# Rotary embedding on one core: two tiles rotated by POOL, eight added by it, five summed by TensorE, and VectorE at full tile width throughout

## The chip, the core and the metric

The kernel runs on one core of a Trainium2 chip. The core has TensorE (PE), VectorE (DVE), ScalarE (ACT), GpSimd (POOL) and SyncE (SP), which run their own instruction streams and wait for one another by semaphores. Data moves between the main memory (HBM), the on-chip memory SBUF and TensorE's accumulators (PSUM); 16 DMA engines carry the HBM traffic. Transfers here are issued from two queues: SP's, shown as q1, and ACT's, shown as q10. The metric is the device time in microseconds of one execution, and the median of several is compared.

## The reference

The input `x` has the shape (8, 8, 1024, 64) in float32, and the tables `cos_cached` and `sin_cached` have the shape (1024, 32). Each row of 64 is rotated as two halves of 32:

```python
x_first, x_second = x[:, :, :, :half], x[:, :, :, half:]
out_first = x_first * cos_cached - x_second * sin_cached
out_second = x_first * sin_cached + x_second * cos_cached
```

An output element is thus a product with the cosine, plus or minus a product of the other half with the sine.

## The kernel before

`x` is cut into 16 tiles, numbered 0 to 15. A tile is 128 partitions by 2048 elements (32 rows of 64), or 1 MB. All tiles have their own place in SBUF (`xt`), and results overwrite them. The loads are issued at once from SP's queue: tiles 0 and 1 alone (L64), then pairs. Before them go the sine table on SP (L57) and the cosine table on ACT (L58). The tables are spread to 128 partitions twice: to PSUM (`snp` by VectorE, `csp` by ScalarE, L72 and L73), where VectorE's products read them, and within SBUF (`sn`, `cs`, by POOL, L76), where POOL's own products read them.

A tile takes one of four ways:

- `on_pool`: POOL does two products (L87, L88) and two half-tile additions (L92, L93), and SP stores.
- `vector_pool`: VectorE does the two products, with the sine product in a `vs` buffer, POOL does the two additions, and SP stores. Tile 12's additions and store are cut in two halves.
- `vector_tensor`: VectorE does the two products; TensorE adds them by multiplying with the identity matrix `plus` and its negative `minus`, into the PSUM tile `acc` (L115, L116), 16 rows at a time; ScalarE copies the sums back to SBUF (L118) and issues the store from ACT's queue.
- `vector_alone`: VectorE does all four operations on half a tile (L132 to L135). Its sine product lies in an `acc` buffer in PSUM, and ACT issues the store.

The order is written out by hand (`manual_schedule`), one call after another; each engine executes its share in that order. `vector_tensor` gets tiles 0, 2, 5, 8 and 11; `on_pool` 1, 6 and 9; `vector_pool` 3, 4, 7, 10 and 12. Tile 13 is split: TensorE sums its first half, and `vector_alone` does its second. Tiles 14 and 15 are `vector_alone`, in halves.

There are six `vs` buffers for the sine products (`tv`), one `gs` buffer for POOL's (`tg`), and two `acc` buffers of 16 rows in PSUM (`pa`). A buffer is written again only when its last readers are done. A store waits for its tile's last writer and, where it uses a semaphore that an earlier transfer had, for that one.

Of the kernel before, what the change touches and what calls it, by code (L numbers as in the profile page):

```python
# [8 lines left out]
@with_exitstack  # L9
def kernel(  # L10
    ctx: ExitStack,
    tc: tile.TileContext,
    x: bass.AP,
    cos_cached: bass.AP,
    sin_cached: bass.AP,
    out: bass.AP,
):
    nc = tc.nc
    fp32 = mybir.dt.float32
    TT = mybir.AluOpType  # L20
    P = nc.NUM_PARTITIONS

    b, h, seq, hd = x.shape
    half = hd // 2
    R = 32
    F = R * hd
    T = R * half
    Q = seq // R
    reps = P // Q
    n_ch = (b * h * seq) // (R * P)  # L30
    G = 512 // half
    assert seq % R == 0 and P % Q == 0 and Q % 32 == 0

    xf = x.rearrange("b h s d -> (b h s d)").rearrange(
        "(c p m) -> c p m", p=P, m=F)
    of = out.rearrange("b h s d -> (b h s d)").rearrange(
        "(c p m) -> c p m", p=P, m=F)

    ctx.enter_context(tc.manual_schedule())
    const = ctx.enter_context(tc.tile_pool(name="const", bufs=1))  # L40
    xp = ctx.enter_context(tc.tile_pool(name="xp", bufs=1))
    tv = ctx.enter_context(tc.tile_pool(name="tv", bufs=6))
    tg = ctx.enter_context(tc.tile_pool(name="tg", bufs=1))
    pt = ctx.enter_context(
        tc.tile_pool(name="pt", bufs=1, space=bass.MemoryType.PSUM))
    pa = ctx.enter_context(
        tc.tile_pool(name="pa", bufs=2, space=bass.MemoryType.PSUM))

    cs = const.tile([P, T], fp32, name="cs")
    sn = const.tile([P, T], fp32, name="sn")  # L50
    plus = const.tile([P, P], fp32, name="plus")
    minus = const.tile([P, P], fp32, name="minus")
    csp = pt.tile([P, T], fp32, name="csp")
    snp = pt.tile([P, T], fp32, name="snp")


    nc.sync.dma_start(out=sn[0:Q], in_=sin_cached.rearrange("(p n) j -> p (n j)", p=Q))  # L57
    nc.scalar.dma_start(out=cs[0:Q], in_=cos_cached.rearrange("(p n) j -> p (n j)", p=Q))  # L58


    xt = []
    for first, n in [(0, 1), (1, 1)] + [(c, 2) for c in range(2, n_ch, 2)]:
        t = xp.tile([P, n, F], fp32, name=f"x{first}")
        nc.sync.dma_start(out=t, in_=xf[first:first + n].rearrange("c p m -> p c m"))  # L64
        xt += [t[:, i] for i in range(n)]

    for t, v in ((plus, 1.0), (minus, -1.0)):
        nc.gpsimd.memset(t, 0.0)
        nc.gpsimd.affine_select(out=t, in_=t, compare_op=TT.not_equal, fill=v,
                                base=0, pattern=[[-1, P]], channel_multiplier=1)  # L70
    for r in range(reps):
        nc.vector.tensor_copy(out=snp[r * Q:(r + 1) * Q], in_=sn[0:Q])  # L72
        nc.scalar.copy(out=csp[r * Q:(r + 1) * Q], in_=cs[0:Q])  # L73
    for t in (sn, cs):
        for r in range(1, reps):
            nc.gpsimd.tensor_copy(out=t[r * Q:(r + 1) * Q], in_=t[0:Q])  # L76

    def rows(t, n0=0, n1=R):
        return t[:, n0 * hd:n1 * hd].rearrange("p (n k j) -> p n k j", k=2, j=half)

    def tab(t, n0=0, n1=R):
        v = t[:, n0 * half:n1 * half].rearrange("p (n o j) -> p n o j", o=1, j=half)
        return v.to_broadcast([P, n1 - n0, 2, half])

    def products(eng, c, s, ctab, stab):
        xr = rows(xt[c])
        eng.tensor_tensor(out=rows(s), in0=xr, in1=tab(stab), op=TT.mult)  # L87
        eng.tensor_tensor(out=xr, in0=xr, in1=tab(ctab), op=TT.mult)  # L88

    def sums(eng, c, s, n0, n1):  # L90
        xr, sr = rows(xt[c], n0, n1), rows(s, n0, n1)
        eng.tensor_tensor(out=xr[:, :, 0], in0=xr[:, :, 0], in1=sr[:, :, 1], op=TT.subtract)  # L92
        eng.tensor_tensor(out=xr[:, :, 1], in0=xr[:, :, 1], in1=sr[:, :, 0], op=TT.add)  # L93

    def store(q, c, n0=0, n1=R):
        q.dma_start(out=of[c][:, n0 * hd:n1 * hd], in_=xt[c][:, n0 * hd:n1 * hd])

    def on_pool(c):
        s = tg.tile([P, F], fp32, name="gs")
        products(nc.gpsimd, c, s, cs, sn)  # L100
        sums(nc.gpsimd, c, s, 0, R)
        store(nc.sync, c)

    def vector_pool(c, cuts=(0, R)):
        s = tv.tile([P, F], fp32, name="vs")
        products(nc.vector, c, s, csp, snp)
        for n0, n1 in zip(cuts, cuts[1:]):
            sums(nc.gpsimd, c, s, n0, n1)
            store(nc.sync, c, n0, n1)

    def tensor_sums(c, s, n0):
        xr, sr = rows(xt[c], n0, n0 + G), rows(s, n0, n0 + G)
        acc = pa.tile([P, 2, G, half], fp32, name="acc")
        for k in range(2):
            nc.tensor.matmul(acc[:, k], plus, xr[:, :, k], start=True, stop=False)  # L115
            nc.tensor.matmul(acc[:, k], plus if k else minus, sr[:, :, 1 - k],  # L116
                             start=False, stop=True)
        nc.scalar.copy(out=xr, in_=acc.rearrange("p k n j -> p n k j"))  # L118

    def vector_tensor(c):  # L120
        s = tv.tile([P, F], fp32, name="vs")
        products(nc.vector, c, s, csp, snp)
        for n0 in range(0, R, G):
            tensor_sums(c, s, n0)
        store(nc.scalar, c)

    def vector_alone(c, n0):
        n1 = n0 + G
        xr = rows(xt[c], n0, n1)
        s = pa.tile([P, 2, G, half], fp32, name="acc")  # L130
        sr = s.rearrange("p k n j -> p n k j")
        nc.vector.tensor_tensor(out=sr, in0=xr, in1=tab(snp, n0, n1), op=TT.mult)  # L132
        nc.vector.tensor_tensor(out=xr, in0=xr, in1=tab(csp, n0, n1), op=TT.mult)  # L133
        nc.vector.tensor_tensor(out=xr[:, :, 0], in0=xr[:, :, 0], in1=s[:, 1], op=TT.subtract)  # L134
        nc.vector.tensor_tensor(out=xr[:, :, 1], in0=xr[:, :, 1], in1=s[:, 0], op=TT.add)  # L135

    vector_tensor(0)
    on_pool(1)
    vector_tensor(2)
    vector_pool(3)  # L140
    vector_pool(4)
    on_pool(6)
    vector_tensor(5)
    vector_pool(7)
    vector_tensor(8)
    on_pool(9)
    vector_pool(10)
    vector_tensor(11)
    vector_pool(12, (0, G, R))


    s = tv.tile([P, F], fp32, name="vs")
    xr, sr = rows(xt[13], 0, G), rows(s, 0, G)
    nc.vector.tensor_tensor(out=sr, in0=xr, in1=tab(snp, 0, G), op=TT.mult)
    nc.vector.tensor_tensor(out=xr, in0=xr, in1=tab(csp, 0, G), op=TT.mult)
    tensor_sums(13, s, 0)
    vector_alone(13, G)
    store(nc.scalar, 13)
    for c in (14, 15):
        for n0 in range(0, R, G):  # L160
            vector_alone(c, n0)
            store(nc.scalar, c, n0, n0 + G)

# [1 line left out]
_INS = ['x', 'cos_cached', 'sin_cached']  # L165
# [26 lines left out]
```

## Time and profile before

| What | Value |
|---|---|
| Median of 4 runs | 86.16 us (85.98 to 86.93) |
| Profiled execution | 85.98 us |
| Its span | 84.0 us |
| Bytes moved | 33.82 MB, mean 402 GB/s over the span |
| PE busy | 42.1 us, 50% |
| VectorE busy | 70.7 us, 84% |
| ACT busy | 16.5 us, 20% |
| POOL busy | 71.7 us, 85% |
| DMA share of q1 and q10 | 72.8% and 24.2% |

The busy times are those of the profiled execution, and the shares are of its span. The span runs from the program's first instruction to its last; the execution's time beside it contains what lies around it. A slice of the span is 2.1 us. The DMA share is the mean busy share of the 16 engines.

### The profile page before, as it was taken

To read this page: it belongs to the slowest core of one execution; us is meant where nothing else is said; L and a number is where in the kernel's file an instruction comes from. 1 tells how busy PE (TensorE), PEld (TensorE's weight loads), DVE (VectorE), ACT (ScalarE), POOL (GpSimd) and SP (SyncE) were. 2 spreads that over 40 slices of the span, in tenths; PEclk is the share of its full clock that TensorE was granted. 3 is DMA by queue.
4 is the path that set the end of the run, shared out by engine and by line. 5 is a ranking of instruction groups with operands and counts; after the bars stand their busy time and mean duration, and the time that the engine had idled before them with its cause. 6 is when DMAs were issued, how large, how long until landed. Compare 5 with 4: busy or idle time off the path is not lost.

```text
span 84.0 us, 396 instructions
## 1 busy us (share of the span) xinstructions
PE 42.1 (50%) x88; PEld 17.6 (21%) x88; DVE 70.7 (84%) x46; ACT 16.5 (20%) x16; POOL 71.7 (85%) x38
## 2 busy tenths in 40 slices
PE   0000007999999708995599829999960000000000
PEld 0000004344444104440344214444400000000000
DVE  0399997999999999999999999990599999999400
ACT  4397000013404220044004130040431000000000
POOL 5399999999999999999999999999999999960000
PEclk9999999999999999999999995699998555555555
DMA  1999999999999999999999999999999999999992
GB/s 41 333 437 433 421 402 433 433 433 406 413 433 316 429 429 417 437 437 429 417 421 437 417 437 437 425 421 421 437 413 437 437 425 421 411 435 409 417 423 88
DMA packets 5024, 33.82 MB, mean 402 GB/s; under 512 B 480, under 2 KB 480, under 8 KB 1312
## 3 DMA queue, kind: packets, MB, share of 16 engines
q1 hardware_dynamic: 3536, 25.30, 72.8%
q10 hardware_dynamic: 1488, 8.52, 24.2%
HBM read 17.04 MB, written 16.78 MB: 402 GB/s over the span
## 4 chain that ended last, share of the span: by engine, by line
PE 46%; DVE 32%; issue 6%; ACT 5%; DMA 3%; DVEq 1%
PE acc L115 24%; PE acc L116 22%; DVE x L133 7%; DVE acc L132 7%; DVE snp L72 6%; ACT x L118 5%; DVE x L134 3%; DMA sn<-in_sin_cached_dram 3%; DVE x L135 3%; DVE vs L87 3%; DVE x L88 3%; DVEq L187 1%; DVEq L88 0%
## 5 line engine op out<-in xcount | busy, mean ns | idle before, releaser
L115 PE MATMUL acc<-x,plus 128*128 128x512 f32 x44 | 24.6, 643 | 20.1 <-DVE x L88 13.2
L87 DVE TENSOR_TENSOR vs<-x,snp 128x2048 f32<-128x2048 f32 x10 | 22.8, 2281 | 0.5 <-DMA x<-in_x_dram 0.5
L88 DVE TENSOR_TENSOR x<-x,csp 128x2048 f32<-128x2048 f32 x10 | 22.9, 2287 | 0.4
L118 ACT COPY x<-acc 128x1024 f32<-128x1024 f32 x11 | 11.1, 1013 | 44.2 <-PE acc L116 44.2
L115 PEld LDWEIGHTS acc<-x,plus 128*128 128x128 f32 x44 | 8.7, 205 | 32.1 <-issue 26.6
L88 POOL TENSOR_TENSOR x<-x,cs 128x2048 f32<-128x2048 f32 x3 | 13.6, 4531 | 0.2
L87 POOL TENSOR_TENSOR gs<-x,sn 128x2048 f32<-128x2048 f32 x3 | 13.6, 4545 | 0.1
L116 PE MATMUL acc<-vs,minus 128*128 128x512 f32 x22 | 12.9, 670 | 0.0
L93 POOL TENSOR_TENSOR x<-x,vs 128x1024 f32<-128x1024 f32 (+1 forms) x6 | 12.0, 1996 | 0.0
L92 POOL TENSOR_TENSOR x<-x,vs 128x1024 f32<-128x1024 f32 (+1 forms) x6 | 11.9, 1992 | 0.0
L116 PE MATMUL acc<-vs,plus 128*128 128x512 f32 x22 | 11.2, 592 | 0.0
L132 DVE TENSOR_TENSOR acc<-x,snp 128x1024 f32<-128x1024 f32 x5 | 6.1, 1225 | 3.1 <-ACT x L118 3.1
L72 DVE COPY snp<-sn 32x1024 f32<-32x1024 f32 x4 | 4.9, 1223 | 3.5 <-DMA sn<-in_sin_cached_dram 3.4
L92 POOL TENSOR_TENSOR x<-x,gs 128x1024 f32<-128x1024 f32 x3 | 7.1, 2352 | 0.2
L93 POOL TENSOR_TENSOR x<-x,gs 128x1024 f32<-128x1024 f32 x3 | 7.1, 2353 | 0.0
L133 DVE TENSOR_TENSOR x<-x,csp 128x1024 f32<-128x1024 f32 x5 | 6.1, 1221 | 0.2
L116 PEld LDWEIGHTS acc<-vs,minus 128*128 128x128 f32 x22 | 4.6, 210 | 6.0 <-issue 6.0
L116 PEld LDWEIGHTS acc<-vs,plus 128*128 128x128 f32 x22 | 4.3, 197 | 5.6 <-issue 5.6
L76 POOL COPY sn<-sn 32x1024 f32<-32x1024 f32 x3 | 3.1, 1032 | 1.8 <-DMA sn<-in_sin_cached_dram 1.7
L73 ACT COPY csp<-cs 32x1024 f32<-32x1024 f32 x4 | 4.0, 1008 | 1.4 <-DMA cs<-in_cos_cached_dram 1.3
L134 DVE TENSOR_TENSOR x<-x,acc 128x512 f32<-128x512 f32 x5 | 3.4, 687 | 0.2
L135 DVE TENSOR_TENSOR x<-x,acc 128x512 f32<-128x512 f32 x5 | 3.4, 679 | 0.0
(12 smaller groups left out, 8.2 us busy)
## 6 DMA issues: line engine op xcount, KB each, us to landing
x<-in_x_dram SPq DMA_DIRECT2D x7, 2048.0 KB, 26.5
out_dram<-x SPq DMA_DIRECT2D x7, 1024.0 KB, 16.2
out_dram<-x ACTq DMA_DIRECT2D x6, 1024.0 KB, 9.0
x<-in_x_dram SPq DMA_DIRECT2D x2, 1024.0 KB, 6.0
out_dram<-x ACTq DMA_DIRECT2D x4, 512.0 KB, 7.1
out_dram<-x SPq DMA_DIRECT2D x2, 512.0 KB, 7.1
cs<-in_cos_cached_dram ACTq DMA_DIRECT2D x1, 128.0 KB, 3.0
sn<-in_sin_cached_dram SPq DMA_DIRECT2D x1, 128.0 KB, 2.7
```

Of the source, the lines that this page charges most:

```text
L72: nc.vector.tensor_copy(out=snp[r * Q:(r + 1) * Q], in_=sn[0:Q])
L87: eng.tensor_tensor(out=rows(s), in0=xr, in1=tab(stab), op=TT.mult)
L88: eng.tensor_tensor(out=xr, in0=xr, in1=tab(ctab), op=TT.mult)
L92: eng.tensor_tensor(out=xr[:, :, 0], in0=xr[:, :, 0], in1=sr[:, :, 1], op=TT.subtract)
L93: eng.tensor_tensor(out=xr[:, :, 1], in0=xr[:, :, 1], in1=sr[:, :, 0], op=TT.add)
L115: nc.tensor.matmul(acc[:, k], plus, xr[:, :, k], start=True, stop=False)
L116: nc.tensor.matmul(acc[:, k], plus if k else minus, sr[:, :, 1 - k], start=False, stop=True)
L118: nc.scalar.copy(out=xr, in_=acc.rearrange("p k n j -> p n k j"))
L132: nc.vector.tensor_tensor(out=sr, in0=xr, in1=tab(snp, n0, n1), op=TT.mult)
L133: nc.vector.tensor_tensor(out=xr, in0=xr, in1=tab(csp, n0, n1), op=TT.mult)
L134: nc.vector.tensor_tensor(out=xr[:, :, 0], in0=xr[:, :, 0], in1=s[:, 1], op=TT.subtract)
L135: nc.vector.tensor_tensor(out=xr[:, :, 1], in0=xr[:, :, 1], in1=s[:, 0], op=TT.add)
```

## The change

The split of the tiles is made anew, and no half-width operation of VectorE is left. `on_pool` gets tiles 1 and 6; `vector_pool` gets 2, 3, 5, 8, 10, 12, 13 and 14, of which 14 is added and stored in two halves; `vector_tensor` gets 0, 4, 7, 9 and 11. Tile 15 is the only one of `vector_alone`, which now works on a whole tile and issues one store of 1 MB from ACT's queue. The two `acc` buffers become one tile of 128x2048 in PSUM, of which TensorE uses one half (16 rows) after the other; tile 15's sine product lies in all of it. `minus` is made by ScalarE from `plus` instead of by POOL. The order in which the loads are issued stays, as do the six `vs` buffers.

```diff
-        tc.tile_pool(name="pa", bufs=2, space=bass.MemoryType.PSUM))
+        tc.tile_pool(name="pa", bufs=1, space=bass.MemoryType.PSUM))
...
+    acc = pa.tile([P, F], fp32, name="acc")
...
-    for t, v in ((plus, 1.0), (minus, -1.0)):
-        nc.gpsimd.memset(t, 0.0)
-        nc.gpsimd.affine_select(out=t, in_=t, compare_op=TT.not_equal, fill=v,
-                                base=0, pattern=[[-1, P]], channel_multiplier=1)
+    nc.gpsimd.memset(plus, 0.0)
+    nc.gpsimd.affine_select(out=plus, in_=plus, compare_op=TT.not_equal, fill=1.0,
+                            base=0, pattern=[[-1, P]], channel_multiplier=1)
+    nc.scalar.mul(minus, plus, -1.0)
...
     def vector_tensor(c):
         s = tv.tile([P, F], fp32, name="vs")
         products(nc.vector, c, s, csp, snp)
         for n0 in range(0, R, G):
-            tensor_sums(c, s, n0)
+            xr, sr = rows(xt[c], n0, n0 + G), rows(s, n0, n0 + G)
+            a = acc[:, n0 * hd:(n0 + G) * hd].rearrange("p (k n j) -> p k n j", k=2, j=half)
+            for k in range(2):
+                nc.tensor.matmul(a[:, k], plus, xr[:, :, k], start=True, stop=False)
+                nc.tensor.matmul(a[:, k], plus if k else minus, sr[:, :, 1 - k],
+                                 start=False, stop=True)
+            nc.scalar.copy(out=xr, in_=a.rearrange("p k n j -> p n k j"))
         store(nc.scalar, c)
 
-    def vector_alone(c, n0):
...
+    def vector_alone(c):
+        products(nc.vector, c, acc, csp, snp)
+        sums(nc.vector, c, acc, 0, R)
+        store(nc.scalar, c)
 
     vector_tensor(0)
     on_pool(1)
-    vector_tensor(2)
+    vector_pool(2)
     vector_pool(3)
-    vector_pool(4)
+    vector_tensor(4)
     on_pool(6)
-    vector_tensor(5)
-    vector_pool(7)
-    vector_tensor(8)
-    on_pool(9)
+    vector_pool(5)
+    vector_tensor(7)
+    vector_pool(8)
+    vector_tensor(9)
     vector_pool(10)
     vector_tensor(11)
-    vector_pool(12, (0, G, R))
...
+    vector_pool(12)
+    vector_pool(13)
+    vector_pool(14, (0, G, R))
+    vector_alone(15)
```

More of the change, by code (lines that the diff above doesn't have):

```diff
@@ L109, in vector_pool @@
             store(nc.sync, c, n0, n1)
[L111 to L118, printed above, removed]
     def vector_tensor(c):
@@ L123, in vector_tensor @@
         for n0 in range(0, R, G):
-            tensor_sums(c, s, n0)
-        store(nc.scalar, c)
-    def vector_alone(c, n0):
[L128 to L135, printed above, removed]
+            xr, sr = rows(xt[c], n0, n0 + G), rows(s, n0, n0 + G)
[5 more added lines that the diff above has]
+            nc.scalar.copy(out=xr, in_=a.rearrange("p k n j -> p n k j"))
+        store(nc.scalar, c)
+    def vector_alone(c):
+        products(nc.vector, c, acc, csp, snp)
+        sums(nc.vector, c, acc, 0, R)
+        store(nc.scalar, c)
     vector_tensor(0)
     on_pool(1)
-    vector_tensor(2)
+    vector_pool(2)
     vector_pool(3)
-    vector_pool(4)
+    vector_tensor(4)
     on_pool(6)
-    vector_tensor(5)
-    vector_pool(7)
-    vector_tensor(8)
-    on_pool(9)
+    vector_pool(5)
+    vector_tensor(7)
+    vector_pool(8)
+    vector_tensor(9)
     vector_pool(10)
     vector_tensor(11)
-    vector_pool(12, (0, G, R))
[L152 to L162, printed above, removed]
+    vector_pool(12)
+    vector_pool(13)
+    vector_pool(14, (0, G, R))
+    vector_alone(15)
 _INS = ['x', 'cos_cached', 'sin_cached']
```

## The prediction

> **What bounds the kernel now.** I read the slices first, then the queues, and only then the engines.
>
> ```profile
> DMA  1999999999999999999999999999999999999992
> GB/s 41 333 437 433 421 402 433 433 433 406 413 433 316 429 429 417 437 437 429 417 421 437 417 437 437 425 421 421 437 413 437 437 425 421 411 435 409 417 423 88
> DMA packets 5024, 33.82 MB, mean 402 GB/s; under 512 B 480, under 2 KB 480, under 8 KB 1312
> ```
>
> The 16 DMA engines are full from the second slice to the last but one. No compute engine looks like that over the whole span. The table of windows shows how the end is reached:
>
> ```profile
> core 0: us, PE busy (x) PEld busy (x) DVE busy (x) ACT busy (x) POOL busy (x), PEclk, DMA share, GB/s
> 28.00:64.00 36.00, 27.29 (x58) 11.00 (x57) 32.57 (x19) 8.10 (x8) 35.69 (x13) 0.95 1.01 427
> 72.00:76.00 4.00, 0.00 (x0) 0.00 (x0) 3.93 (x5) 0.00 (x0) 2.82 (x3) 0.50 1.02 425
> 76.00:80.00 4.00, 0.00 (x0) 0.00 (x0) 2.56 (x4) 0.00 (x0) 0.00 (x0) 0.50 1.02 417
> ...
> 81.00:82.00 1.00, 0.00 (x0) 0.00 (x0) 0.00 (x0) 0.00 (x0) 0.00 (x0) 0.50 1.02 418
> 82.00:83.00 1.00, 0.00 (x0) 0.00 (x0) 0.00 (x0) 0.00 (x0) 0.00 (x0) 0.50 0.40 160
> ```
>
> VectorE, the last engine to work, stops at 78.6 us, but the DMA engines stay full until 82.5 us. The last landing is at 83.08 us, and 0.95 us of closing work completes the span of 84.03 us. The steady rate is 427 GB/s, or 0.427 MB per us. The 33.82 MB alone need 79 us of it. The change moves exactly the same bytes. So it can gain next to nothing while the queues stay fed, and it loses where it leaves them empty.
>
> The chain of waits says otherwise, and is the view to distrust here:
>
> ```profile
> PE 46%; DVE 32%; issue 6%; ACT 5%; DMA 3%; DVEq 1%
> ```
>
> It follows compute instructions back from VectorE's last one, and cannot show that their stores waited in a full queue.
>
> **The unit prices.**
>
> ```profile
> L87 DVE TENSOR_TENSOR vs<-x,snp 128x2048 f32<-128x2048 f32 x10 | 22.8, 2281 | 0.5 <-DMA x<-in_x_dram 0.5
> L88 DVE TENSOR_TENSOR x<-x,csp 128x2048 f32<-128x2048 f32 x10 | 22.9, 2287 | 0.4
> L87 POOL TENSOR_TENSOR gs<-x,sn 128x2048 f32<-128x2048 f32 x3 | 13.6, 4545 | 0.1
> L134 DVE TENSOR_TENSOR x<-x,acc 128x512 f32<-128x512 f32 x5 | 3.4, 687 | 0.2
> ```
>
> In the timeline VectorE takes a new tile's products every 4.52 us (two operations that overlap by 0.05). POOL takes a whole tile in 13.8 us (10.03 to 23.84) and the two additions of a tile in 4.6 us (46.95 to 51.55).
>
> **POOL: three whole tiles and five tiles of sums become two and eight.** Removed: one whole tile, 13.8 us. Added: three times 4.6, also 13.8. Before, POOL's tile work ran from 10.03 to 74.81; it still ends at about 74.8. Its order becomes 1, 2, 3, 6, 5, 8, 10, 12, 13, 14: adds end at 51.55 (tile 5), 56.15, 60.75, 65.35, 69.95, and tile 14's halves at 72.4 and 74.8. The unneeded memset and select for `minus` (0.5 us) end before POOL's wait for `sn` at 3.5, so taking them away gives nothing.
>
> **ScalarE: makes `minus` by one 128x128 multiplication.** No such row exists. Between 0 and the 1.01 us of the 128x1024 copy, I take 0.3. It falls between the table load's end at 2.46 and the cosine table's landing at 3.75; if it overran, `csp` at 7.9 would still be 2.9 us ahead of its first use at 10.85. Cost 0.
>
> **TensorE: five and a half tiles of sums become five.** Half a tile goes: four matmuls in two passes each, 8 x 0.43 = 3.4 us in the timeline, and one 1.01 us copy. With it goes VectorE's wait for that copy:
>
> ```profile
> 59.85 1.23 DVE L132 TENSOR_TENSOR acc<-x,snp 128x1024 f32<-128x1024 f32 x1 [3.08 <-ACT x L118]
> ```
>
> From the end of a product to the issue of its ACT store takes 8.2 us (31.79 to 40.07), 10.0 where the clock was halved (49.87 to 59.85). The single `acc` with two halves holds as much PSUM as the two buffers did. Tiles 4, 7 and 9 are ready at 27.25, 36.3 and 45.3, so PE is free before each: no new wait.
>
> **VectorE: 14 full products and one addition.** Gone are five half-width groups of four operations and one half-width pair. Tile 0 runs as before, to 13.14; tile 2 starts at 13.62. Then 2, 3, 4, 5, 7, 8, 9, 10 follow every 4.52 us, and tile 11 would start at 49.78. It does not. There are six `vs` buffers, and in the built program tile 11's first product waits for POOL's last addition of tile 5, whose buffer it takes over. POOL reaches that here:
>
> ```profile
> 46.95 2.34 POOL L92 TENSOR_TENSOR x<-x,vs 128x1024 f32<-128x1024 f32 x1
> 49.24 2.34 POOL L93 TENSOR_TENSOR x<-x,vs 128x1024 f32<-128x1024 f32 x1
> 51.55 4.52 POOL L87 TENSOR_TENSOR gs<-x,sn 128x2048 f32<-128x2048 f32 x1
> ```
>
> So the change adds a wait of 1.8 us. The balance: removed are 5 x 3.75 for the half-width groups, 2.45 for the pair and the wait of 3.08, 24.3 in all; added are four tiles of 4.52, two additions of about 1.2 (below) and 1.8, 22.3 in all. VectorE comes out 2.0 earlier. Behind it stand tiles 11 to 15 on VectorE; PE's sums of 11 and POOL's of 12 to 14 wait for those. Products of 11, 12, 13, 14 and 15 then end at 56.1, 60.6, 65.1, 69.65 and 74.2. POOL wants 12 at 60.75, 13 at 65.35 and 14 at 69.95, so it gets each just in time. Tile 15's two additions over 128x1024 have no row; the 128x512 ones repeat every 0.60 us, the 128x1024 multiplication every 1.24, so between 1.1 and 1.25 each, I take 1.2. VectorE ends at 76.6 instead of 78.63, and the last store is issued at 76.65.
>
> Here a rule speaks against the change. The Trainium skill, SBUF - State Buffer, "Who interferes with whom", says a VectorE instruction with two SBUF inputs and a GpSimd instruction reading SBUF exclude one another for a whole instruction. If tile 15's two additions stood behind POOL's last ones, 1.27 each, they would end up to 2.5 us later, at 79.1. Their second input is `acc` in PSUM, however, and the row of the same kind did not block:
>
> ```profile
> 69.90 1.28 POOL L92 TENSOR_TENSOR x<-x,vs 128x512 f32<-128x512 f32 x1
> 69.92 0.69 DVE L134 TENSOR_TENSOR x<-x,acc 128x512 f32<-128x512 f32 x1
> ```
>
> I take 0.
>
> **Stores: what the DMA engines have left.** Nineteen stores become 17. The Trainium skill, DMA: Bandwidth & Descriptors, "Anatomy of one DMA", gives about 2.0 us fixed per DMA; two fewer in series would save 4 us. The DMA share of 1.0 says that these fixed parts lie under other transfers, so I take 0. Only the tail's 417 instead of 425 GB/s, where 4 KB rows dominate, may improve: 6.5 us x 2% = 0.13 us. The slower stretch before the first store's bytes (375 GB/s in 24:28, some 0.5 us) stays, for that store is unchanged.
>
> SP's stores stand in one queue behind the loads. Each can also wait for an older transfer that used its semaphore: for 10, 12, 13 and 14 that is the store of 1, 2, 3 and then 6 and 5, landed at about 66 at the latest, an estimate from the order of bytes at 427 GB/s. No wait comes from there.
>
> In the packet records a store's first byte moves 3.5 to 3.9 us after its issue (23.06 to 26.99, 49.11 to 52.63, 59.85 to 63.48); I use 3.6. At each such moment I compare all bytes offered earlier with what the full engines had moved in the old trace. Tile 10: 27.53 MB offered, 26.16 moved. Tile 11 (issued at 64.3): 28.57 against 27.66. Tile 13: 30.67 against 30.09. Second half of 14: 32.24 against 32.12. Tile 15, first byte at 76.65 + 3.6 = 80.25: 32.77 against 32.90, short by 0.13 MB, or 0.3 us. So the engines stay fed until 79.9, and the last 1.05 MB then run alone: 80.25 + 1.05/0.427 = 82.7, against 82.5 before.
>
> **Sum.** +0.2 for the last store, -0.1 for larger rows: +0.1. The profiled execution took 85.98 us (1.95 beside its span), giving 86.1. The median of four runs is 86.16, 0.2 above it, giving 86.3. I predict 86.2. A measurement of this kernel can tell about 1% from no change, so this is no change.
>
> **Rivals.**
>
> *The last store ends late (slower).* Place: VectorE's handover at tile 11 and the one-piece store of tile 15. Against before, where the last store was half a megabyte, the end is now issue + 3.6 + 2.46, one for one with VectorE. It decides once the store is issued after 76.45, and costs 1% from 77.3. With VectorE 0.5 us later and the longest latency of 3.93: 77.15 + 3.93 + 2.46 = 83.5, 1.0 over before; 87.2 us. For it: POOL's margins of 0.15 to 0.3 us, and the median of 9.0 us to landing of a 1 MB ACT store. Against: that median is from stores that shared the engines, and the wait's length is fixed by rows which do not change. 22%.
>
> *The end follows the engines (faster).* If the chain of waits were right, VectorE's 2.0 us would come off: 84.2 on the median. Against: 33.82 MB at 427 cannot end before about 82 us. Even regaining the 0.5 us dip and the tail gives 85.4 to 85.6, under 1%. 5%.
>
> *The change does not do what it says.* In the built order POOL, TensorE and VectorE have exactly the tiles named above. 0.
>
> **How the numbers follow.** No change 73%, slower 22%, faster 5%. The range goes down to 85.4 (dip and tail regained) and up to 87.3, to hold most of the slower case.
>
> **What would show it.** Right: VectorE idle 1.8 us before tile 11, releaser POOL; VectorE's end near 76.6; POOL's near 74.8; DMA share 1.0 until about 79.9; last bytes at 82.3 to 83.0. Wrong: a DMA share under 0.9 in any window between 30 and 78, VectorE ending after 77.3, or a span that falls with VectorE's end.

## The result, and the profile after

The changed kernel takes 85.90 us (median of 43 runs, 85.75 to 86.69), the kernel before 86.23 us (64 runs, 85.83 to 87.12). The ratio is 0.9959, with a 95% interval of 0.9947 to 0.9972. No change was forecast (86.2 us, +0.1). The time lies inside the forecast range, but the gain of 0.33 us is clear of the noise, and the prediction did not have it.

The profiled execution does not show the gain. It took 86.09 us with a span of 84.3, where the one of before took 85.98 with 84.0. From the page after, the slices and the DMA packets, as shown for before:

```profile
DMA  1999999999999999999999999999999999999991
GB/s 39 346 420 424 428 420 420 428 431 416 416 420 431 284 431 428 428 416 420 431 431 435 432 428 431 412 420 435 428 431 431 428 431 412 424 431 416 433 437 43
DMA packets 4736, 33.82 MB, mean 401 GB/s; under 512 B 448, under 2 KB 448, under 8 KB 768
```

The bytes are the same to the digit, the mean rate is 401 instead of 402 GB/s, and the packets under 8 KB are fewer (768 for 1312). The stretch before the first store's bytes has moved by a slice, and its slice is a little poorer (284 for 316). The windows at the end of the changed kernel:

```profile
core 0: us, PE busy (x) PEld busy (x) DVE busy (x) ACT busy (x) POOL busy (x), PEclk, DMA share, GB/s
72.00:76.00 4.00, 0.00 (x0) 0.00 (x0) 3.93 (x4) 0.00 (x0) 2.83 (x3) 0.50 1.01 428
76.00:78.00 2.00, 0.00 (x0) 0.00 (x0) 0.74 (x1) 0.00 (x0) 0.00 (x0) 0.50 0.95 399
...
81.00:82.00 1.00, 0.00 (x0) 0.00 (x0) 0.00 (x0) 0.00 (x0) 0.00 (x0) 0.50 0.97 410
82.00:83.00 1.00, 0.00 (x0) 0.00 (x0) 0.00 (x0) 0.00 (x0) 0.00 (x0) 0.50 0.47 197
```

VectorE ends 2 us earlier, at 76.7 us, but the last byte goes at 82.96 us (82.6 before). The queues run a little short between 76 and 78 us (share 0.95), then they are full again. The timeline of VectorE shows the new wait before tile 11 and the last two additions, with POOL's last one and the issue of the last store among them:

```profile
51.54 2.29 DVE L88 TENSOR_TENSOR vs<-x,snp 128x2048 f32<-128x2048 f32 x1 [1.71 <-POOL x L94]
...
73.54 1.29 POOL L94 TENSOR_TENSOR x<-x,vs 128x512 f32<-128x512 f32 x1
74.39 1.22 DVE L93 TENSOR_TENSOR x<-x,acc 128x1024 f32<-128x1024 f32 x1
...
75.53 1.21 DVE L94 TENSOR_TENSOR x<-x,acc 128x1024 f32<-128x1024 f32 x1
76.77 0.34 ACTq L97 DMA_DIRECT2D out_dram<-x  x1
```

One wait was not foreseen. The table of waits of the changed kernel has:

```profile
engine line waited for: us in total, times, longest us
...
PE acc L119 <- ACT x L122: 8.8, 8, 1.1
...
DVE vs L88 <- POOL x L94: 1.7, 1, 1.7
```

TensorE's half tiles no longer follow one another directly. Each waits for ScalarE's copy of the half before, so a half takes 4.80 us instead of 3.43. Tile 11's store is issued at 67.4 us instead of the 64.3 of the prediction's sum. The DMA engines were not short of bytes for it: their share was 1.01 from 28 to 64 us, 1.02 to 72 and 1.01 to 76.

### The profile page after: what moved, and what is told of

The parts are those of the page before. It is cut to its first block, busy times and chain, and to the rows that moved or that the text cites. A ratio compares the mean times of both kernels' runs of the same rounds, so it can differ in the third digit from the quotient of the medians.

```text
span 84.3 us, 363 instructions
## 1 busy us (share of the span) xinstructions
PE 41.1 (49%) x80; PEld 15.9 (19%) x80; DVE 70.4 (84%) x34; ACT 15.7 (19%) x16; POOL 71.4 (85%) x38
## 2 busy tenths in 40 slices
DMA packets 4736, 33.82 MB, mean 401 GB/s; under 512 B 448, under 2 KB 448, under 8 KB 768
## 4 chain that ended last, share of the span: by engine, by line
POOL 53%; DVE 23%; issue 9%; DMA 3%; DVEq 1%; POOLq 0%
POOL x L94 13%; POOL x L93 11%; DVE vs L88 11%; POOL x L89 11%; POOL gs L88 11%; DVE x L89 8%; POOL sn L77 4%; POOL cs L77 3%; DMA sn<-in_sin_cached_dram 3%; DVE acc L88 3%; DVE x L93 1%; DVEq L170 1%; POOLq L93 0%; POOLq L77 0%
## 5 line engine op out<-in xcount | busy, mean ns | idle before, releaser
L89 DVE TENSOR_TENSOR x<-x,csp 128x2048 f32<-128x2048 f32 x14 | 32.0, 2287 | 0.6
L88 DVE TENSOR_TENSOR vs<-x,snp 128x2048 f32<-128x2048 f32 x13 | 29.7, 2281 | 2.2 <-POOL x L94 1.7
L94 POOL TENSOR_TENSOR x<-x,vs 128x1024 f32<-128x1024 f32 (+1 forms) x9 | 19.1, 2126 | 0.0
L93 POOL TENSOR_TENSOR x<-x,vs 128x1024 f32<-128x1024 f32 (+1 forms) x9 | 19.1, 2118 | 0.0
L119 PEld LDWEIGHTS acc<-x,plus 128*128 128x128 f32 x40 | 7.6, 210 | 38.5 <-issue 23.0
L89 POOL TENSOR_TENSOR x<-x,cs 128x2048 f32<-128x2048 f32 x2 | 9.1, 4540 | 0.2
L88 POOL TENSOR_TENSOR gs<-x,sn 128x2048 f32<-128x2048 f32 x2 | 9.1, 4534 | 0.1
L93 POOL TENSOR_TENSOR x<-x,gs 128x1024 f32<-128x1024 f32 x2 | 4.7, 2352 | 0.2
L94 POOL TENSOR_TENSOR x<-x,gs 128x1024 f32<-128x1024 f32 x2 | 4.7, 2356 | 0.0
L77 POOL COPY cs<-cs 32x1024 f32<-32x1024 f32 x3 | 3.1, 1034 | 0.1
L88 DVE TENSOR_TENSOR acc<-x,snp 128x2048 f32<-128x2048 f32 x1 | 2.3, 2297 | 0.0
L93 DVE TENSOR_TENSOR x<-x,acc 128x1024 f32<-128x1024 f32 x1 | 1.2, 1220 | 0.0
```

Source lines behind the costliest of these rows:

```text
L119: nc.tensor.matmul(a[:, k], plus, xr[:, :, k], start=True, stop=False)
```

## The experiments

Every run lists its time and its span, so the time **beside the span** is known for each, and not only for the profiled one. The runs of the kernel before that an experiment lists were made on the same chip as the experiment.

**1. Is it TensorE's clock and VectorE's wait for it?** The old kernel's runs scatter upwards (to 87.1) and the new one's do not. In the old kernel VectorE waits for ScalarE's copy of TensorE's sums, and the halved clock of TensorE lengthens that wait. Theory A: such runs end late, and the change removed the dependence. Theory B: fewer and larger stores gain it. The first run exchanges two calls of the kernel before:

```diff
-    vector_pool(10)
-    vector_tensor(11)
+    vector_tensor(11)
+    vector_pool(10)
```

> The kernel before with only the calls for tiles 10 and 11 exchanged, so that TensorE sums tile 11 one place (4.5 us) earlier and VectorE no longer waits 3.1 us for ScalarE's copy before tile 13's second half; some 0.7 us of wait may be left at tile 14. All stores keep number and size. Theory A (the old kernel's last stores hang on TensorE by that wait, whose length changes from run to run): VectorE ends near 76.3 us, median 85.8 to 86.0 us, ratio 0.995 to 0.998, and the upper runs (86.5 and more) go. Theory B (the gain is in the data movement: fewer and larger stores): ratio 0.999 to 1.001, spread as before.

Measured: 86.38 us, ratio 1.0033 (1.0011 to 1.0054). VectorE ended at 76.6 instead of 78.6, with a wait of 0.9 us:

```profile
57.84 1.23 DVE L132 TENSOR_TENSOR acc<-x,snp 128x1024 f32<-128x1024 f32 x1 [0.91 <-ACT x L118]
```

The second run keeps the order and gives TensorE work where it idled:

```diff
     vector_tensor(8)
+    idle = pa.tile([P, 2, G, half], fp32, name="acc")
+    for k in range(2):
+        nc.tensor.matmul(idle[:, k], plus, cs[:, 0:512], start=True, stop=True)
     on_pool(9)
```

> The kernel before with two more fp32 matmuls (128x512, into an acc buffer that is overwritten afterwards) after tile 8's sums, so that TensorE has no idle 1.9 us at 48 us and keeps its clock. Nothing else changes. Theory A with the clock as the cause of the changing wait: granted clock 1.0 from 17 to 62 us, VectorE's wait before tile 13's second half 1.2 to 1.5 us instead of 3.1, VectorE's end 1.6 us earlier, ratio 0.995 to 0.998. Theory B: ratio 0.999 to 1.001 although the wait is shorter.

Measured: 86.54 us, ratio 1.0044 (1.0018 to 1.0069). The granted clock stayed at 1.0 from 35 to 66 us (a stretch of 0.5 lay earlier, at 31.8 to 35.2), and the wait was the expected one:

```profile
58.23 1.23 DVE L132 TENSOR_TENSOR acc<-x,snp 128x1024 f32<-128x1024 f32 x1 [1.38 <-ACT x L118]
```

Both kernels took 1.6 to 2 us from VectorE's end and gained nothing; they are 0.3 and 0.4% slower, and why is open. The late runs stayed: time beside the span of 2.4 us or more in 9 of 22 and 7 of 22 runs. Theory A falls.

**2. Does the last store set the end?** This tests the prediction's sum from both sides, in the changed kernel.

```diff
-    tv = ctx.enter_context(tc.tile_pool(name="tv", bufs=6))
+    tv = ctx.enter_context(tc.tile_pool(name="tv", bufs=7))
```

> The changed kernel with seven vs buffers instead of six, so that VectorE does not wait 1.7 us for POOL before tile 11. The prediction's sum: the last store is issued at 75.0 instead of 76.77, the DMA engines are not short of bytes at its start, last byte 82.5 or a little earlier instead of 82.96, some 0.3 to 0.5 us: ratio to the kernel before 0.990 to 0.993. Theory B: the end is set by the bytes alone, 0.995 to 0.997 as without this edit.

Measured: 85.98 us, ratio 0.9959 (0.9943 to 0.9976), the same as without the edit; the expected 0.990 to 0.993 is missed. VectorE's wait was gone, and the last store was issued at 75.22 us instead of 76.77:

```profile
75.22 0.34 ACTq L97 DMA_DIRECT2D out_dram<-x  x1
```

The other side:

```diff
+    spare = const.tile([P, T], fp32, name="spare")
+    for r in range(2):
+        nc.vector.tensor_copy(out=spare, in_=csp)
     vector_alone(15)
```

> The changed kernel with two copies of a table (128x1024 each, PSUM to SBUF, into a spare tile) on VectorE ahead of tile 15: 2.4 us of work that nothing else needs. The prediction's sum (the last store stands alone: issue + 3.6 + 2.46): VectorE ends near 79.2, last byte near 85.3, 2.3 us later, about 88.2 us, ratio 1.02 to 1.03. If the last store still had cover in the queues, the ratio would stay under 1.01.

Measured: 86.25 us, ratio 0.9989 (0.9970 to 1.0009), not the 1.02 to 1.03 of the sum. The last store was issued at 79.52, 2.75 us later than in the changed kernel, and the mean span grew from 84.16 us (with seven buffers, same chip) to 84.44. The issue and the windows of this run:

```profile
79.52 0.34 ACTq L97 DMA_DIRECT2D out_dram<-x  x1
...
78.00:80.00 2.00, 0.00 (x0) 0.00 (x0) 1.49 (x2) 0.00 (x0) 0.00 (x0) 0.50 0.97 397
80.00:81.00 1.00, 0.00 (x0) 0.00 (x0) 0.00 (x0) 0.00 (x0) 0.00 (x0) 0.50 0.72 299
81.00:82.00 1.00, 0.00 (x0) 0.00 (x0) 0.00 (x0) 0.00 (x0) 0.00 (x0) 0.50 1.08 442
82.00:83.00 1.00, 0.00 (x0) 0.00 (x0) 0.00 (x0) 0.00 (x0) 0.00 (x0) 0.50 0.76 311
```

Before the last bytes go at 83.0 us, only the window at 80 shows a gap. In the packet records this store's first byte moves at 80.37, that is 0.85 us after its issue, against 3.2 us (76.77 to 79.97) in the changed kernel. So most of the 3.6 us of the prediction's sum is time behind the bytes queued ahead of a store. When the engines run out of bytes that part vanishes, and a late store is nearly as good as an early one. A shift of VectorE by 4.3 us between these two runs moves the time by 0.27 us.

**3. Where is the gain, then?** On one chip the means over all runs are:

| Kernel (runs) | Time | Span | Beside the span |
|---|---|---|---|
| before (75) | 86.29 | 84.23 | 2.06 |
| changed, seven `vs` buffers (22) | 85.96 | 84.16 | 1.80 |

The changed kernel's own 44 runs (the 43 above and one more) have the same means, 84.16 and 1.80. Of 0.33 us, 0.26 lie outside the span, where no view of the profile looks; the other 0.07 are a shorter span, and what makes it shorter was not tested. The old kernel had 1.9 to 2.0 us in 58 of these 75 runs and 2.4 to 2.6 in 17. The changed kernel had 1.7 to 1.9 in all of its 44. Theory C: this comes with the length of an engine's instruction stream, that is, the list of instructions that the engine executes. VectorE has 60 instructions in the built program before and 48 after, ScalarE 48 and 40, TensorE 58 and 53 (88 and 80 matmuls in the profile). SyncE's stream became longer (42 and 46 instructions in the traces); no run varies it. Theory D: it comes with ACT's stores, 10 before and 6 after. Four runs lengthen one thing each in the changed kernel, where the engine is idle:

```diff
+    tiny = const.tile([P, 12], fp32, name="tiny")
+    for i in range(12):
+        nc.vector.memset(tiny[:, i:i + 1], 0.0)
     vector_tensor(11)
```

> The changed kernel with 12 one-column memsets of a spare tile on VectorE, placed in its 1.7 us wait before tile 11, so that its stream has as many instructions as before (60 instead of 48). Open is where 0.15 to 0.3 us per execution went that no span shows: the time beside the span is 1.8 us in the changed kernel, 1.95 (in a quarter of the executions 2.4 to 2.6) in the kernel before and its two variants. Theory C (it comes with the length of an engine's instruction stream, here VectorE's): 1.95 with some at 2.5, median 86.0 to 86.2. If VectorE's stream is not the one: 1.8, and 85.9.

```diff
+    tiny = const.tile([P, 8], fp32, name="tiny")
+    for i in range(8):
+        nc.scalar.copy(out=tiny[:, i:i + 1], in_=plus[:, i:i + 1])
     vector_tensor(4)
```

> The changed kernel with 8 one-column copies on ScalarE into a spare tile, placed where it is idle before tile 4, so that its stream has 48 instructions as before instead of 40. Theory C with ScalarE's stream: time beside the span 1.95 with some at 2.5, median 86.0 to 86.2. If it is another engine's, or not code at all: 1.8, and 85.9.

```diff
+    for i in range(4):
+        nc.tensor.matmul(acc[:, 0:P], plus, plus, start=True, stop=True)
     vector_tensor(4)
```

> The changed kernel with four more matmuls (128x128, into a half of acc that is overwritten afterwards) before tile 4, where TensorE is idle, so that it runs 88 matmuls as before instead of 80. Theory C with TensorE's stream: time beside the span 1.95 with some at 2.5, median 86.0 to 86.2. If it is another engine's, or not code at all: 1.8, and 85.9.

```diff
-        store(nc.scalar, c)
+        cuts = (0, 10, 20, R) if c in (0, 4) else (0, R)
+        for n0, n1 in zip(cuts, cuts[1:]):
+            store(nc.scalar, c, n0, n1)
```

> The changed kernel with the stores of tiles 0 and 4 each issued from ACT's queue in three parts, so that ACT issues 10 stores as before instead of 6; all other work is the same. Theory D (the time beside the span comes with the number of stores issued on ACT's queue): 1.95 with some at 2.5. Theory C: 1.8 unless ScalarE's stream, 46 instructions here, is the cause, which the run with copies tells apart. Smaller rows here should cost the span under 0.1 us, since the queues are full then.

| Run | Runs | Median | Ratio (95%) | Beside the span, median | Late (about 2.4 or more) |
|---|---|---|---|---|---|
| 12 on VectorE | 20 | 86.11 | 0.999 (0.9977 to 1.0003) | 1.92 | 0 |
| 8 on ScalarE | 20 | 85.96 | 0.9962 (0.9944 to 0.9981) | 1.79 | 0 |
| 4 matmuls | 12 | 85.88 | 0.9947 (0.9923 to 0.9970) | 1.78 | 0 |
| 10 stores on ACT | 8 | 85.98 | 0.9967 (0.9941 to 0.9993) | 1.81 | 0 |
| before, same chip | 51 | 86.19 | | 1.92 | 9 |

VectorE's filler alone brings back the 1.92, and the span did not grow (84.2). The twelve stand in the wait, at no cost of their own:

```profile
50.08 0.20 DVE L143 MEMSET tiny<- 128x1 f32 x12
51.83 2.29 DVE L88 TENSOR_TENSOR vs<-x,snp 128x2048 f32<-128x2048 f32 x1 [1.54 <-POOL x L94]
```

Theory D falls, and so do ScalarE's and TensorE's streams taken alone; the spare tile is not the cause either, since ScalarE's run has one too. The late executions did not come back, however.

**4. Length, or place? And the late ones?** The same fillers, combined, and VectorE's doubled (`range(24)`):

> The changed kernel with the three fillers at once: 12 memsets on VectorE in its wait before tile 11, 8 copies on ScalarE and 4 small matmuls on TensorE, both where these are idle. The instruction streams are about as long as in the kernel before (60, 47 and 57 instructions; before 60, 48 and 58). Theory C in full (both the 0.12 us and the late executions of the old kernel come with the length of the streams): time beside the span 1.92, in about a fifth of the executions 2.4 to 2.6, median 86.0 to 86.2. Theory C for VectorE alone: 1.92 in all, no late ones; then the late ones have another cause, such as the stores' pattern at the end.

> The changed kernel with the fillers of VectorE and ScalarE (60 and 48 instructions, TensorE's stream as changed). If the late executions need these two streams: 1.92 with a fifth at 2.4 to 2.6. If they need TensorE's, or have another cause: 1.92 in all.

> The changed kernel with the fillers of VectorE and TensorE (60 and 57 instructions, ScalarE's stream as changed). If the late executions need these two streams: 1.92 with a fifth at 2.4 to 2.6. If they need ScalarE's, or have another cause: 1.92 in all.

> The changed kernel with 24 instead of 12 memsets on VectorE in the same wait (72 instructions). If the time beside the span grows with the length of VectorE's stream in proportion: 2.05. If 0.12 us is a step that lies between 50 and 60 instructions: 1.92 again. The span should stay at 84.1 to 84.2.

Measured in 12 runs each, all four on one chip:

| Run | Median | Ratio (95%) | Span | Beside | Late |
|---|---|---|---|---|---|
| all three fillers | 86.22 | 0.9973 (0.9947 to 0.9999) | 84.3 | 1.94 | 0 |
| VectorE and ScalarE | 86.17 | 0.9973 (0.9946 to 1.0) | 84.25 | 1.91 | 0 |
| VectorE and TensorE | 86.23 | 0.9995 (0.997 to 1.0019) | 84.3 | 1.90 | 2 (2.5 and 2.6) |
| VectorE doubled | 86.24 | 0.9976 (0.9954 to 0.9999) | 84.45 | **1.80** | 0 |

With 72 instructions neither expected value came (2.05 or 1.92), and the span is longer by 0.15 to 0.2 us than in the three runs with 60. So the time beside the span does not grow with the length. The next guess, still theory C, is that it depends on where the stream ends. The first two ratios lie just clear of 1, a hint that part of the gain stays when the twelve instructions are back.

The trace holds the DMA packets that fetch instructions too. With 72 instructions there is one such packet of 8192 bytes inside the span, at 67.37 us; the changed kernel has none after its start. The packets do not say for which engine they are. The profiled executions of the two variants in point 1 were late ones (3.5 and 2.6 us beside the span). Both have a 16384-byte fetch after the span's end, at 86.67 and 85.99 us. The profiled execution of the kernel before was not late, and shows none.

If this is the cause, a longer stream must help the kernel before. In its 3 us wait there is room:

```diff
+    tiny = const.tile([P, 12], fp32, name="tiny")
+    for i in range(12):
+        nc.vector.memset(tiny[:, i:i + 1], 0.0)
     vector_alone(13, G)
```

> The kernel before with 12 one-column memsets of a spare tile on VectorE, in its 3 us wait ahead of tile 13's second half (72 instructions instead of 60). Theory C (where VectorE's stream ends decides the time beside the span): 1.8 instead of 1.95 and no executions at 2.4 to 2.7, so that more instructions make it faster, ratio 0.995 to 0.998. Rival (the late executions belong to the old kernel's stores or other engines): late ones as before, in a fifth; ratio 0.999 to 1.001.

With `range(24)` in its place:

> The kernel before with 24 such memsets in the same wait (84 instructions). Theory C: as with 12, 1.8 and no late executions, unless the length meets the next unlucky position. Rival: late ones as before, ratio 0.999 to 1.001.

And two lengths between, in the changed kernel (`range(6)` and `range(18)`):

> The changed kernel with 6 memsets on VectorE in its wait before tile 11 (54 instructions). Theory C has the unlucky position somewhere from 51 to 71 instructions: 1.8 or 1.92, which bounds it from below. If the time beside the span moved smoothly with length: 1.86.

> The changed kernel with 18 memsets on VectorE in its wait before tile 11 (66 instructions). Theory C: 1.8 or 1.92, which bounds the position from above; late executions only if it is 1.92.

| Run | VectorE's instructions | Median | Span | Beside | Late | Fetch seen in the trace |
|---|---|---|---|---|---|---|
| changed (44 runs) | 48 | 85.90 | 84.1 | 1.79 | 0 | none |
| changed + 6 (12) | 54 | 86.04 | 84.2 | 1.79 | 0 | none |
| changed + 12 (20) | 60 | 86.11 | 84.2 | 1.92 | 0 | none |
| changed + 18 (12) | 66 | 86.05 | 84.4 | 1.66 | 0 | at 84.98, after the end |
| changed + 24 (12) | 72 | 86.24 | 84.45 | 1.80 | 0 | at 67.37 |
| before (35) | 60 | 86.19 | 84.2 | 1.93 | 6 | none |
| before + 12 (12) | 72 | 86.24 | 84.4 | 1.80 | 0 | at 65.19 |
| before + 24 (12) | 84 | 86.29 | 84.5 | 1.80 | 0 | at 65.40 |

Each entry of the last column is from one profiled execution. Twelve more instructions take the 0.13 us and the late executions out of the kernel before, as theory C has it. The ratio did not follow: 1.0004 (0.9984 to 1.0023) instead of 0.995 to 0.998, because the span grows by 0.2 us. The filler itself does not cost that; it lies inside the wait:

```profile
56.90 0.21 DVE L159 MEMSET tiny<- 128x1 f32 x12
58.33 1.23 DVE L132 TENSOR_TENSOR acc<-x,snp 128x1024 f32<-128x1024 f32 x1 [1.22 <-ACT x L118]
```

So at 72 and 84 instructions the time beside the span is shorter, the span is longer by about as much, and the kernel before is no faster for it. Whether that is one cost that moved, or two, is not shown. At 66 instructions the time beside is 1.66, neither of the two expected values. The span is longer by 0.2 us than at 54 and the time beside it shorter by 0.13, so that the two medians are equal (86.05 and 86.04, one chip). Here the trace shows where the span grew. VectorE's last instruction, a semaphore at the end of the program, ends at 84.34 us, 0.16 after ScalarE's:

```profile
L173 DVEq EVENT_SEMAPHORE  x2: 21/21/21, 83.7 to 84.3; - x2
L173 ACTq EVENT_SEMAPHORE  x2: 17/17/17, 83.7 to 84.2; - x2
```

In every other trace of the study the two end within 0.02 us of each other. The last byte is as early at 66 as at 54 (82.76 and 82.79). So at 66 the border between the span and the rest has moved, and no time was lost. No kernel of the study beats the changed one clearly: the best ratio, 0.9947 with the four matmuls, has an interval that overlaps its own.

Shown by these runs: VectorE's instruction count moves the median time beside the span (60 against 48, 54, 66 and 72 in the changed kernel, 60 against 72 and 84 in the one before). Single runs are less clean: in the kernel before, 2 of 12 at 72 and 4 of 12 at 84 still had 1.96 to 2.15.

Shown beside it: the late executions have only been seen with 60 instructions. There were 40 in 196 runs of the kernel before, 16 in 44 of its two variants in point 1 and 2 in 56 of the changed kernel at 60, but none in 138 at 48 to 54, none in 24 of the changed kernel at 66 and 72 and none in 24 of the kernel before at 72 and 84. So 60 instructions alone are not enough for them: something else of the kernel before takes part.

Argued only: that a fetch of instructions is the carrier. VectorE's late last instruction at 66 speaks for it. Two things speak against the simple form, in which a fetch belongs to a fixed place in VectorE's stream. At 60 the trace ends without a fetch in the common case. And in the kernel before, the fetch comes at 65.19 us with 72 instructions and at 65.40 with 84, after 53 and 65 of VectorE's traced instructions; with twelve more ahead of it, it should have come twelve instructions earlier in the work.

Open: what else the late executions need, and why the span is 0.15 to 0.3 us longer at 72 and 84.

## Why the prediction was right or wrong

**The bound was right.** The kernel moves 33.82 MB through full DMA engines. VectorE's 2 us shortened the span by 0.07 us at most (mean 84.23 before, 84.16 in the seven-buffer version on the same chip), and the rival in which the end follows the engines is refuted: two kernels with VectorE 1.6 to 2 us earlier gained nothing.

**The engines' steps were right.** VectorE waited 1.71 us before tile 11 (1.8 forecast) and the last store was issued at 76.77 (76.65). SP issued the store of tile 14's last half at 74.86 (74.8). ScalarE's `minus` took 0.31 us (0.3). Tile 15's additions took 1.22 and 1.21 (1.2) and did not stand behind POOL: the one at 74.39 began while POOL's of 73.54 was running. The rule on two SBUF inputs did not apply to them, as taken.

**The step that failed is the first line of the sum**: "The profiled execution took 85.98 us (1.95 beside its span)". The 1.95 was carried over as a constant, and the change was put at nothing there. It is a term of its own, and the change moves it: the median is 1.80 instead of 1.92 to 1.95, and the late executions are gone, which in the mean are worth another 0.13 us (17 of 75, 0.57 us each). Between the forecast of +0.1 and the measured -0.33, this term makes 0.26 of 0.43 us; the rest is the span, forecast at +0.1 and measured at -0.07.

The 0.13 of the median comes from twelve instructions fewer on VectorE: the filler of twelve brings it back. The prediction counted removed instructions by their busy time alone. The late executions do not come back with the twelve (2 of 56); they leave the kernel before when its count changes (0 of 24), so the count has a part in them, and the rest of their cause stays open.

The Trainium skill, Runtime: NRT & Kernel Launch, "Instruction fetch mechanics", says that streams are fetched in blocks while the engine runs and that crossing a block is mostly hidden. The trace at 72 instructions agrees: with a fetch at 67.37, VectorE's next product starts at 67.78, 2.32 us after the one before, as elsewhere. That the 0.13 us at 60 is what is left of such a crossing is not shown.

**The term for the last store had the wrong slope.** "Issue + 3.6 + 2.46", one for one with VectorE, gave +0.2 us. The slower rival rested on it with 22%. A store issued 2.75 us later cost 0.3 us, because the first byte then needs 0.85 us and not 3.6. The old trace already held a sign of it: the 3.6 is from three earlier stores, while its last store was issued at 78.67 and moved its first byte at 81.10, 2.4 us later. In the profiled pair the last byte did come 0.34 us later (82.62 before in the packet records, not the 82.5 of the sum), but the spans of all runs show no such loss.

**The fixed part of a store was quoted from the wrong case.** The section of the Trainium skill that the prediction quotes for it (DMA: Bandwidth & Descriptors, "Anatomy of one DMA") gives its 2.0 us for transfers that GpSimd issues. The stores here come from SP and ACT, and no run isolates their fixed part. The step taken from it, no gain from two fewer stores, does not rest on the figure.

**"PE is free before each: no new wait" was wrong.** It took the two halves of `acc` for two independent buffers. TensorE waited for ScalarE's copy of the other half eight times, 1.10 us each. That it cost nothing fits the DMA share, which stayed at 1.01 or more until 76 us; no run removes this wait.

**One profiled execution stood for too much.** The one of before had a span 0.2 us under its mean, the one after 0.14 over. The pair says +0.11 us, as forecast, and that agreement is chance; the populations say -0.33. With as many runs as here, a measurement tells far less than the prediction's 1% from no change: the interval of the ratio is 0.25% wide.

## What to carry to other kernels

When the DMA engines are full, moving an engine's end by some microseconds in either direction is worth tenths at most, so look for the cost of a store in the queue ahead of it and not in a fixed latency. For effects under 1%, split every run's time into the span and what lies beside it before looking for a cause in the trace: here three quarters of the gain was outside all views. The number of an engine's instructions can move the time beside the span although their busy time buys nothing: here 48 instead of 60 on VectorE were worth 0.13 us. Fewer is not better as a rule: with 66 and 72 the time beside the span was also shorter than with 60, and the span longer by about as much. So before a gain of some tenths of a percent is put down to a kernel's design, fill an engine's idle time with small instructions and see whether the gain stays.

## What the runs showed of the hardware that was not expected

The delay from the issue of a store on ACT's queue to its first byte was 3.4 to 4.1 us with full queues, 2.4 to 3.7 for the last store of the two kernels and of the seven-buffer version, and 0.85 us once the queues had drained. The median time beside the span was 1.66, 1.80 or 1.92 us, depending on how many instructions VectorE executes, and single executions near 2.5 us occurred only with 60. Instruction fetches share the DMA engines' records with the data, and can be found there by their kind and size.
